# A block of attention, a state-space mixer and 32 experts: the first gather issued ahead of the low parts, masks behind the first four reciprocal roots

## The chip, the cores and the metric

The kernel runs on one core of a Trainium2 chip, in one launch. The metric is device time in microseconds (us). The five engines of the core are TensorE (PE in the profile), VectorE (DVE), ScalarE (ACT), GpSimd (POOL) and SyncE (SP, which here only issues loads); each runs its own list of instructions in order, and waits on semaphores for the others.

## The reference

The input is `x`, 1024 rows of 1024 numbers in float32. Cut to what is computed:

```python
h = rmsnorm(x, norm_mix_g)
q, k, v, f, u_ssm, g_attn, g_ssm = split(h @ w_in)         # 512 512 512 8 512 1024 1024
y_attn = forgetting_attention(rmsnorm(q), rmsnorm(k), v, f + b_forget)   # 8 heads of 64
y_ssm = s5(u_ssm, ...)                                     # 32 groups, state 64, GELU, GLU
mixed = sigmoid(g_attn) * (y_attn @ w_proj_attn) + sigmoid(g_ssm) * (y_ssm @ w_proj_ssm)
x = x + mixed @ w_out
xt = rmsnorm(x, norm_ffn_g)
# router: the best of 4 groups, in it the best 2 of 8 experts, weights renormalised
for e in range(32):
    y += combine[:, e:e+1] * ((silu(xt @ w_gate[e]) * (xt @ w_up[e])) @ w_down[e])
return x + y
```

Each expert has two matrices of 1024 x 256 and one of 256 x 1024, in all 3 MB in float32.

## The kernel before, in words

**Products.** Most products are made of three: a float32 operand is cast to a high part (ScalarE, names ending in `h`), and VectorE subtracts that from the operand to get the low part (names ending in `l`). TensorE then multiplies high by high, high by low and low by high into the same PSUM tile.

**The start (lines 95 to 262).** SyncE loads `x` in eight tiles of 128 rows, the first four ahead of `raw_u` (the weights of `u_ssm` and `f`, four loads), the last four (`xs2`) behind it. `normalize` (L176) takes four tiles: ScalarE squares and sums a tile (L180), VectorE makes the mean square `ss` (L181), GpSimd raises it to -1/2 (`rstd`, L183), VectorE scales the tile (L184). `split_u` (L193) makes `wuh`, `wul` and a small `wf`, which GpSimd clears first (L227). `turn_x` (L186) transposes four tiles on TensorE and splits the result into `hTh` (ScalarE, L190) and `hTl` (VectorE, L191). For the first half of the rows this stands in a manual schedule for ScalarE and VectorE; on the other engines, and elsewhere, a scheduler orders the instructions from their dependencies. The masks `tri`, `mask_s`, `mask_m` and three small vectors (L232 to L254) are made on GpSimd wherever it comes to them. The second half's `normalize(xs2)` is placed behind the last `hTl` of the first half by `tc.issue_after`, which orders instructions of one engine.

**The routing.** The last large product before the experts, `mixed @ w_out`, goes over 16 units (a tile of 128 rows, one half of the columns). Behind each unit `tail` (L1169) does the routing of a finished tile, mostly in small instructions of VectorE: best group, best two experts, and from comparisons and small products on TensorE a table `ptab` of which rows each expert takes. At the end VectorE writes `ix` (L1313), the row numbers of each of the 32 experts, 96 places each, and `wts` (L1314). The normalised rows go to a scratch tensor `xn_d` in HBM. `AHEAD` (L1126) says in which unit which loads of weights are issued: an expert has four loads of `raw_e` and two of `wd`, 512 KB each, in five sets of buffers, so that expert 5's `raw_e` waits until expert 0's buffers are read.

**The experts (from L1319).** `gather_rows` fetches an expert's rows from `xn_d` by `ix` into a tile `XG` with an indirect DMA that GpSimd issues (L1330); `XG` is cleared beforehand (`rows_tile`, L1321). `turn_rows` transposes the rows on TensorE (L1341) and splits them into `xh` and `xl` (L1344, L1345). `split_expert` splits an expert's gate and up weights into eight pieces, `weh` on ScalarE (L1103) and `wel` on VectorE (L1104). `gate_up` multiplies (L1354 to L1356), `hidden` applies SiLU (L1362), `down` multiplies by `wd` (L1379), scales (L1380) and adds the rows to the output with an indirect DMA (L1381). The three `XG` are used in turn; gather o + 2 is issued while expert o is multiplied.

Of the kernel before, what the change touches and what calls it, by code (L numbers as in the profile page):

```python
# [19 lines left out]
P = 128  # L20
# [22 lines left out]
def hybrid_block(ctx: ExitStack, tc: tile.TileContext, t, out):  # L43
# [132 lines left out]
    def normalize(xs):  # L176
        for x_ in xs:
# [5 lines left out]
            nc.gpsimd.tensor_tensor(rstd, ss, mhalf[:, 0:1], ALU.pow)  # L183
            nc.vector.tensor_scalar(x_, x_, rstd, None, op0=ALU.mult)  # L184

    def turn_x(xs, k, hs):  # L186
# [3 lines left out]
        nc.scalar.activation(hTh[k][:, hs], ps, AF.Copy, scale=gmix[:, k:k + 1])  # L190
        return nc.vector.scalar_tensor_tensor(hTl[k][:, hs], ps, gmix[:, k:k + 1], f32(hTh[k][:, hs]),  # L191
# [41 lines left out]
    tri = cp.tile([P, P], F32, name="tri")  # L233
    nc.gpsimd.memset(tri, 1.0)
    nc.gpsimd.affine_select(tri, tri, pattern=[[1, P]], compare_op=ALU.is_gt, fill=0.0,
                            base=0, channel_multiplier=-1)

    mask_s = cp.tile([P, 256], BF16, name="mask_s")
    nc.gpsimd.memset(mask_s, 0.0)
    nc.gpsimd.affine_select(mask_s, mask_s, pattern=[[1, 256]], compare_op=ALU.is_ge, fill=NEG,  # L240
                            base=-128, channel_multiplier=-1)

    mask_m = cp.tile([P, P], BF16, name="mask_m")
    nc.gpsimd.memset(mask_m, 0.0)
    nc.gpsimd.affine_select(mask_m, mask_m, pattern=[[-1, P]], compare_op=ALU.is_ge, fill=NEG,
                            base=0, channel_multiplier=1)
    bfor = cp.tile([H, 1], F32, name="bfor")
    nc.gpsimd.dma_start(bfor, t["b_forget"].rearrange("(p o) -> p o", o=1))

    gk2 = cp.tile([P, 1], F32, name="gk2")  # L250
    gqt = cp.tile([P, 1], F32, name="gqt")
    for o in (0, 64):
        nc.gpsimd.dma_start(gk2[o:o + 64], t["k_norm_g"].rearrange("(p o) -> p o", o=1))
        nc.gpsimd.dma_start(gqt[o:o + 64], t["q_norm_g"].rearrange("(p o) -> p o", o=1))  # L254
    xs = xs2
    pu, pf = [mmtile() for _ in range(4)], smtile()
    with tc.issue_after(first_half.ins):
# [833 lines left out]

    def split_expert(raws, c):
# [425 lines left out]
```

## Time and profile before

| | us |
|---|---|
| median of three runs | 1182.69 |
| the three runs | 1181.40, 1182.69, 1185.41 |
| the profiled execution, its own time | 1180.84 |
| its span in the trace | 1179.2 |
| TensorE busy | 1106.0 (94%) |
| VectorE busy | 804.9 (68%) |
| ScalarE busy | 620.3 (53%) |
| GpSimd busy | 356.9 (30%) |

The span runs from the first to the last instruction; 1.6 us of the execution lie around it. The mean granted clock of TensorE is 0.98 of full speed. Busy times overlap between engines. A time within the span is counted from its start.

### The profile page before, as it was taken

The numbers are of one execution on the slowest core, as the hardware profiler recorded it, in microseconds if no ns is written. First come the engines' busy times: TensorE is split into PE (matmuls) and PEld (weight loads), VectorE is DVE, ScalarE is ACT, GpSimd is POOL, SyncE is SP. The second block draws the span as 40 slices with busy tenths as digits, with TensorE's granted clock in tenths as the row PEclk, the third lists the DMA queues.
The fourth block names the chain that finished last, engine by engine and source line by source line (L and its number), as shares of the span: only waits on it lengthen the run. The fifth ranks groups of instructions, "written<-read, shape, count | busy, mean of one in ns | idle before, by whom it ended". The sixth has DMA issues, their size and how long they took to land. (4 is left out here: it accounts for less than half of the span.)

```text
span 1179.2 us, 15928 instructions
## 1 busy us (share of the span) xinstructions
PE 1106.0 (94%) x5323; PEld 848.4 (72%) x5324; DVE 804.9 (68%) x1593; ACT 620.3 (53%) x1195; POOL 356.9 (30%) x399
## 2 busy tenths in 40 slices
PE   5999999999999999999899979997699999999995
PEld 4778878887897888788677868885466666666562
DVE  4986887964247899898986795529466666666660
ACT  5443233234246666658868452204376776666662
POOL 3110111013144565647443451102322222222211
PEclk9999999999999999999999999998799999999998
DMA  7625553321604030002523548554599999999992
GB/s 237 88 75 149 130 82 82 81 73 49 152 22 55 11 64 11 16 10 81 205 81 135 184 170 295 181 208 183 188 331 345 327 315 305 314 317 322 311 331 56
DMA packets 100918, 193.78 MB, mean 164 GB/s; under 512 B 26176, under 2 KB 55168, under 8 KB 100832
## 3 DMA queue, kind: packets, MB, share of 16 engines
q1 hardware_dynamic: 82176, 150.16, 41.5%
q0 software_dynamic: 14048, 34.17, 10.6%
q10 hardware_dynamic: 4608, 8.39, 1.9%
q8 instruction: 43, 0.70, 0.2%
q14 instruction: 43, 0.35, 0.1%
HBM read 164.30 MB, written 35.52 MB: 169 GB/s over the span
## 5 line engine op out<-in xcount | busy, mean ns | idle before, releaser
L1104 DVE TENSOR_TENSOR wel<-raw_e,weh 128x512 fp32r<-128x512 f32 x256 | 157.5, 686 | 116.9 <-ACT weh L1103 116.9
L1103 ACT CAST weh<-raw_e 128x512 fp32r<-128x512 f32 x256 | 137.2, 622 | 2.2 <-DVE wel L1104 0.8
L1379 PE MATMUL psA_t<-wd,hT 128*96 128x512 f32 x256 | 115.7, 594 | 3.0 <-DMA wd<-in_w_expert_down 2.2
L912 POOL TENSOR_TENSOR sm<-sm,pe 128x256 f32<-128x256 f32 (+2 forms) x80 | 96.1, 1202 | 70.3 <-ACT pe L909 62.0
L1354 PE MATMUL psA_t<-weh,xh 128*96 128x512 f32 x256 | 103.8, 406 | 0.2
L1355 PE MATMUL psA_t<-wel,xh 128*96 128x512 f32 x256 | 102.2, 399 | 0.0
L1356 PE MATMUL psA_t<-weh,xl 128*96 128x512 f32 x256 | 101.3, 396 | 0.0
L162 PE MATMUL psA_t<-hTl,wgh 128*128 128x512 f32 x256 | 100.7, 393 | 0.0
L161 PE MATMUL psA_t<-hTh,wgl 128*128 128x512 f32 x256 | 100.7, 393 | 0.0
L160 PE MATMUL psA_t<-hTh,wgh 128*128 128x512 f32 x256 | 100.5, 393 | 0.0
L795 PE MATMUL psA_t<-wqh,hTh 128*128 128x384 f32 x256 | 88.0, 344 | 0.0
L796 PE MATMUL psA_t<-wql,hTh 128*128 128x384 f32 x256 | 86.4, 338 | 0.0
L797 PE MATMUL psA_t<-wqh,hTl 128*128 128x384 f32 x256 | 86.3, 337 | 0.0
L1381 POOL DMA_INDIRECT out_rows<-R,ix x32 | 46.0, 1438 | 127.3 <-ACT hT L1370 116.1
L1380 ACT ACTIVATE R<-psA_t,wts 96x512 f32<-96x512 f32 x64 | 43.7, 682 | 75.8 <-PE psA_t L1379 73.7
L1379 PEld LDWEIGHTS psA_t<-wd,hT 128*96 128x96 f32 x256 | 40.0, 167 | 55.0 <-issue 48.9
L1330 POOL DMA_INDIRECT XG<-xn_d,ix x32 | 35.8, 1119 | 139.0 <-PE psB_t L1341 133.1
L907 ACT ACTIVATE pH<-psB_t 128x512 fp32r<-128x512 f32 (+1 forms) x96 | 49.1, 511 | 36.4 <-PE psB_t L904 36.2
L910 DVE TENSOR_TENSOR pL<-pe,pH 128x256 fp32r<-128x256 f32 (+2 forms) x80 | 62.5, 793 | 6.5 <-ACT pe L909 5.7
L164 ACT COPY ge<-psA_t 128x512 f32<-128x512 f32 x32 | 18.7, 584 | 86.6 <-PE psA_t L162 81.8
L857 DVE TENSOR_REDUCE mx<-psB_t 128x1 f32<-128x512 f32 (+2 forms) x96 | 51.2, 551 | 6.2 <-PE psB_t L855 2.7
L1163 PE MATMUL psA_t<-woh,mxh 128*128 128x512 f32 x128 | 54.3, 424 | 1.2 <-DVE gt L988 1.2
(425 smaller groups left out, 2828.7 us busy)
## 6 DMA issues: line engine op xcount, KB each, us to landing
raw_e<-in_w_expert_gate SPq DMA_DIRECT2D x64, 512.0 KB
raw_e<-in_w_expert_up SPq DMA_DIRECT2D x64, 512.0 KB
wd<-in_w_expert_down SPq DMA_DIRECT2D x64, 512.0 KB
gate_d<-ge ACTq DMA_DIRECT2D x32, 256.0 KB
gt<-gate_d SPq DMA_DIRECT2D x16, 512.0 KB
raw_g<-in_w_in SPq DMA_DIRECT2D x12, 512.0 KB
raw_q<-in_w_in SPq DMA_DIRECT2D x48, 128.0 KB
x<-in_x SPq DMA_DIRECT2D x8, 512.0 KB
```

The lines of the kernel that those rows point to most:

```text
L160: nc.tensor.matmul(ps, wh, hTh[k][:, ns], start=(k == 0), stop=False)
L161: nc.tensor.matmul(ps, wl, hTh[k][:, ns], start=False, stop=False)
L162: nc.tensor.matmul(ps, wh, hTl[k][:, ns], start=False, stop=(k == KD - 1))
L795: nc.tensor.matmul(ps[:, :384], ah, wh, start=(k == 0), stop=False)
L796: nc.tensor.matmul(ps[:, :384], ah, wl, start=False, stop=False)
L912: nc.gpsimd.tensor_tensor(sm[:, o0:], sm[:, o0:], pe[:, :n], ALU.add)
L1103: nc.scalar.copy(wh[d_], src)
L1104: nc.vector.tensor_tensor(wl[d_], src, f32(wh[d_]), ALU.subtract)
L1354: nc.tensor.matmul(ps, xh[:, k, :], wh[:, k % 2, :], start=(k == 0), stop=False)
L1355: nc.tensor.matmul(ps, xh[:, k, :], wl[:, k % 2, :], start=False, stop=False)
L1356: last = nc.tensor.matmul(ps, xl[:, k, :], wh[:, k % 2, :], start=False, stop=(k == KD - 1))
L1379: pe = nc.tensor.matmul(po, hT[:, j, :], wd[j][:, ns], start=(j == 0), stop=(j == 1))
```

## The change

At the start:

- The clearing of `wf` and everything on GpSimd from `tri` to `gqt` is put behind the fourth `rstd` (`power`).
- `normalize(xs2)` is put behind the last `hTh` of the first half too, so that on ScalarE its four Squares come after all eight `hTh`.

At the border between routing and experts:

- `XG[0]` and `XG[1]` are cleared in unit 8 of the product loop instead of after it.
- Expert 2's two `wd` loads are issued after the loop instead of in unit 8.
- Expert 0's weights are split by a function of its own, `split_first`: all eight `weh` first, then `wel` in two groups of four. The first group stands behind `tick`, a one-column tile that GpSimd clears between gather 0 and gather 1 and VectorE copies onto itself; the second stands behind the second `xl` of expert 0's rows.

```diff
 def normalize(xs):
-            nc.gpsimd.tensor_tensor(rstd, ss, mhalf[:, 0:1], ALU.pow)
+            power = nc.gpsimd.tensor_tensor(rstd, ss, mhalf[:, 0:1], ALU.pow)
             nc.vector.tensor_scalar(x_, x_, rstd, None, op0=ALU.mult)
+        return power
...
-        normalize(xs)
-        nc.gpsimd.memset(f32(wf), 0.0)
+        power = normalize(xs)
+        with tc.issue_after(power.ins):
+            nc.gpsimd.memset(f32(wf), 0.0)
...
-            first_half = turn_x(xs, k, halves[0])
+            first_act, first_half = turn_x(xs, k, halves[0])
+    with tc.issue_after(power.ins):
...    (tri, mask_s, mask_m, bfor, gk2, gqt as before, indented)
-    with tc.issue_after(first_half.ins):
+    with tc.issue_after(first_half.ins), tc.issue_after(first_act.ins):
         normalize(xs)
...
+    def split_first(raws, c):
+        ws, low = [], []
+        for k2 in range(4):
+            v = (2 * c + k2 // 2) % 3, k2 % 2
+            ws_t[v] = slot("weh", (2, 512), F32R), slot("wel", (2, 512), F32R)
+            wh, wl = ws_t[v]
+            for q in range(2):
+                src = raws[k2 // 2 * 2 + q][:, k2 % 2 * 2:k2 % 2 * 2 + 2, :]
+                d_ = (slice(None), slice(None), slice(q * 256, q * 256 + 256))
+                nc.scalar.copy(wh[d_], src)
+                low.append((wl[d_], src, f32(wh[d_])))
+            ws.append((wh, wl))
+        for u in range(2):
+            yield ws
+            for l_ in low[4 * u:4 * u + 4]:
+                nc.vector.tensor_tensor(*l_, ALU.subtract)
+        yield ws
...
-    AHEAD = {0: [(0, 6)], 2: [(1, 6)], 8: [(2, 6)], 12: [(3, 6), (4, 2)], 14: [(4, 2)]}
+    AHEAD = {0: [(0, 6)], 2: [(1, 6)], 8: [(2, 4)], 12: [(3, 6), (4, 2)], 14: [(4, 2)]}
...
+            if u == 8:
+                rows_tile(SR)
+                rows_tile(SR)
...
         for _ in range(2):
+            next(ahead[2])
+        for _ in range(2):
             r_ = next(ahead[4])
...
-    rows_tile(SR)
-    rows_tile(SR)
...
-    for o in range(2):
-        last_gather = gather_rows(XG[o], icol(o))
+    tick = em_.tile([P, 1], F32, name="tick")
+    gather_rows(XG[0], icol(0))
+    nc.gpsimd.memset(tick, 0.0)
+    last_gather = gather_rows(XG[1], icol(1))
     with tc.issue_after(last_gather.ins):
         rows_tile(em_)
+    last_dve = nc.vector.tensor_copy(tick, tick)
...
-    with after(ends["act"], last_dve):
-        *_, ws = split_expert(got[0][0], 0)
+    with after(ends["act"]):
+        sp = split_first(got[0][0], 0)
+        ws = next(sp)
+    with after(last_dve):
+        next(sp)
+    x, _, dve = turn_rows(XG[0])
+    with after(dve):
+        next(sp)
     load(5, 4)
-    x, _ = turn_rows(XG[0])
```

`turn_x` and `turn_rows` now return the instructions that the new orders name (`act`, `dve`).

**GpSimd at the start.** The rows stand in the order of the engine; `x4` is four in a row. Before:

```order
L183 TENSOR_TENSOR rstd<-ss,mhalf 128x1
L234 MEMSET tri 128x128
L239 MEMSET mask_s 128x256
L235 AFFINE_SELECT tri<-tri 128x128
L240 AFFINE_SELECT mask_s<-mask_s 128x256
L244 MEMSET mask_m 128x128
L248 DMA bfor<-in_b_forget 8x1
```

and now:

```order
masks.py:199 AFFINE_SELECT ident<-ident 128x128
L183 TENSOR_TENSOR rstd<-ss,mhalf 128x1 x4
L229 MEMSET wf 128x1024
L237 MEMSET tri 128x128
L242 MEMSET mask_s 128x256
L238 AFFINE_SELECT tri<-tri 128x128
```

Before, masks and small DMAs lay between the roots, and the clearing of `wf` ahead of the first one; now the four roots follow each other, and the clearing of `wf` is the next instruction behind them.

**ScalarE at the start.** `x_109` to `x_115` are the four tiles of the second half, `hTh_136` to `hTh_141` the high parts of k = 2 to 7. Before:

```order
L190 ACTIVATE hTh_136<-psB_t,gmix 128x512
L180 ACTIVATE junk,ss<-x_109 128x1024
L190 ACTIVATE hTh_137<-psB_t,gmix 128x512
L180 ACTIVATE junk,ss<-x_111 128x1024
L198 CAST wuh<-raw_u 128x1024
L199 CAST wf<-raw_u 128x2x8
L190 ACTIVATE hTh_138<-psB_t,gmix 128x512
```

and now:

```order
L191 ACTIVATE hTh_136<-psB_t,gmix 128x512
L191 ACTIVATE hTh_137<-psB_t,gmix 128x512
L199 CAST wuh<-raw_u 128x1024
L200 CAST wf<-raw_u 128x2x8
L191 ACTIVATE hTh_138<-psB_t,gmix 128x512
```

The Square of `x_109` stood between the high parts of k = 2 and k = 3; now k = 3 follows k = 2 at once, and the four Squares stand behind `hTh_141`.

**VectorE from the list of rows to the first hidden values `hh`.** Before:

```order
L1313 TENSOR_TENSOR ix<-psA_t,empty 96x32
L1314 COPY wts<-psA_t 96x32
L1104 TENSOR_TENSOR wel<-raw_e,weh 128x2x256 x9
L1345 TENSOR_TENSOR xl<-psB_t,xh 128x384
L1104 TENSOR_TENSOR wel<-raw_e,weh 128x2x256
```

and now:

```order
L1346 TENSOR_TENSOR ix<-psA_t,empty 96x32
L1347 COPY wts<-psA_t 96x32
L1490 TENSOR_REDUCE nblk<-cnt 1x1
L1495 CAST cnti<-cnt 1x32
L1492 TENSOR_SCALAR nblk<-nblk 1x1
L1493 TENSOR_SCALAR nblk<-nblk 1x1
L1496 CAST cnti<-nblk 1x1
L1433 COPY tick<-tick 128x1
L1111 TENSOR_TENSOR wel<-raw_e,weh 128x2x256 x4
L1370 TENSOR_TENSOR xl<-psB_t,xh 128x384 x2
L1111 TENSOR_TENSOR wel<-raw_e,weh 128x2x256 x4
L1126 TENSOR_TENSOR wel<-raw_e,weh 128x2x256 x4
```

The nine `wel` behind `wts` became four, and these stand behind the copy of `tick`; the other four of expert 0 (L1111) stand behind both `xl`, and all four first ones of expert 1 (L1126) behind them. Five small operations on the experts' counts, which stood behind expert 1's `wel` before, now stand ahead of the tick. On GpSimd the same place now reads:

```order
L1304 TENSOR_TENSOR xn_8066<-xn_8066,gfB 128x512
L1355 DMA XG<-xn_d,ix 96x1024
L1429 MEMSET tick 128x1
L1355 DMA XG<-xn_d,ix 96x1024
L1158 MEMSET XG 128x1024
```

Before, the two clearings of `XG` stood between `xn` and the gathers, and the gathers of experts 0 and 1 followed each other.

On SyncE's queue the four `wd` loads (two of expert 2, two of expert 4) now stand between `xn_d` and the loads of expert 5, the first of them between the two halves of `xn_d`; before there were two, behind both halves.

## Rows read from the trace of the kernel before

**Rows 1.** The page of the profile, its first part: busy time of an engine, its share of the span, and its instructions.
```profile
PE 1106.0 (94%) x5323; PEld 848.4 (72%) x5324; DVE 804.9 (68%) x1593; ACT 620.3 (53%) x1195; POOL 356.9 (30%) x399
```

**Rows 2.** The table of windows over the border between routing and experts and over the experts. Columns: the window, its length, busy time and instructions of TensorE (PE), its weight loads (PEld), VectorE (DVE), ScalarE (ACT) and GpSimd (POOL), then the granted clock of TensorE as a share of full speed, the mean busy share of the 16 DMA engines, and what they moved in GB/s.
```profile
820.00:825.00 5.00, 1.54 (x7) 0.92 (x6) 4.34 (x26) 5.00 (x11) 0.63 (x1) 0.50 0.72 218
825.00:830.00 5.00, 0.00 (x0) 0.00 (x0) 3.99 (x7) 0.30 (x1) 4.97 (x1) 0.50 0.68 219
830.00:835.00 5.00, 0.00 (x0) 0.00 (x0) 0.00 (x0) 0.00 (x0) 2.92 (x3) 0.50 0.89 279
835.00:840.00 5.00, 3.52 (x13) 2.61 (x14) 2.02 (x4) 2.51 (x5) 0.96 (x1) 0.50 0.25 71
840.00:845.00 5.00, 5.00 (x18) 3.38 (x17) 1.35 (x7) 0.66 (x1) 0.00 (x0) 0.73 0.78 243
845.00:850.00 5.00, 4.88 (x27) 3.74 (x26) 2.95 (x6) 3.68 (x9) 0.95 (x1) 1.00 0.24 73
...
870.00:900.00 30.00, 30.00 (x127) 18.79 (x126) 18.58 (x34) 20.91 (x43) 7.24 (x6) 1.00 1.03 348
900.00:1100.00 200.00, 200.00 (x836) 125.30 (x835) 124.14 (x219) 139.39 (x278) 47.05 (x40) 1.00 0.99 318
```

**Rows 3.** The timeline of TensorE at the border. Columns of this and of all timelines below: start, duration, engine, line, operation, output<-inputs, shape, number of instructions, and in brackets the idle time before it with what ended it.
```profile
836.43 1.52 PE L1341 MATMUL psB_t<-ident,XG 96*128 96x96 f32 x8 [13.17 <-DMA XG<-xn_d,ix]
...
842.98 0.39 PE L1354 MATMUL psA_t<-weh,xh 128*96 128x512 f32 x1
```

**Rows 4.** The timeline of GpSimd at the border.
```profile
817.10 1.93 POOL L1323 MEMSET XG<- 128x1024 f32 x2
824.37 5.60 POOL L1330 DMA_INDIRECT XG<-xn_d,ix  x1 [5.34 <-DVE wel L1104]
830.27 0.99 POOL L1330 DMA_INDIRECT XG<-xn_d,ix  x1 [0.30 <-DMA raw_e<-in_w_expert_up]
...
838.23 0.96 POOL L1330 DMA_INDIRECT XG<-xn_d,ix  x1 [4.76 <-PE psB_t L1341]
```

**Rows 5.** The timeline of VectorE at the border: the list of rows, the burst of low parts, and the low part of the gathered rows.
```profile
823.30 0.19 DVE L1313 TENSOR_TENSOR ix<-psA_t,empty 96x32 int32<-96x32 f32 x1 [0.60 <-PE psA_t L1265]
...
823.50 5.49 DVE L1104 TENSOR_TENSOR wel<-raw_e,weh 128x512 fp32r<-128x512 f32 x9
837.98 0.56 DVE L1345 TENSOR_TENSOR xl<-psB_t,xh 128x384 fp32r<-128x384 f32 x1 [8.99 <-ACT xh L1344]
```

**Rows 6.** The timeline of VectorE a little earlier: the same comparison `at` for the last tile, first beside the clearings on GpSimd, then alone.
```profile
817.50 0.64 DVE L1264 TENSOR_SCALAR at<-iocap,pos 128x96 f32<-128x96 f32 x1
...
822.36 0.27 DVE L1264 TENSOR_SCALAR at<-iocap,pos 128x96 f32<-128x96 f32 x1
```

**Rows 7.** The instructions of line 1330, the gather, with the time from issue to landing: the first line is of the window that holds the first gather alone, the next two of the 29 from 836 on (durations in ns).
```profile
DMA to landing us min/median/max: 11.9/11.9/11.9
...
L1330 POOL DMA_INDIRECT XG<-xn_d,ix x29: 952/975/991, 838.2 to 1115.8; - x29
...
DMA to landing us min/median/max: 4.0/7.7/8.7
```

**Rows 8.** The timeline of SyncE's queue (SPq) at the border: loads of `wd` and of `raw_e`, 512 KB each.
```profile
819.08 0.83 SPq L1089 DMA_DIRECT2D wd<-in_w_expert_down  x2
825.41 0.33 SPq L1085 DMA_DIRECT2D raw_e<-in_w_expert_gate  x1
...
828.42 0.33 SPq L1085 DMA_DIRECT2D raw_e<-in_w_expert_up  x1
840.27 0.33 SPq L1085 DMA_DIRECT2D raw_e<-in_w_expert_gate  x1
```

**Rows 9.** The timeline of GpSimd at the start.
```profile
2.68 0.98 POOL L227 MEMSET wf<- 128x1024 f32 x1
...
12.15 0.52 POOL L254 DMA_DIRECT2D gqt<-in_q_norm_g  x1
12.69 0.57 POOL L183 TENSOR_TENSOR rstd<-ss,mhalf 128x1 f32<-128x1 f32 x1
```

**Rows 10.** The timeline of VectorE at the start: the mean square and the scaling of the fourth tile of x.
```profile
11.97 0.15 DVE L181 TENSOR_SCALAR ss<-ss 128x1 f32<-128x1 f32 x1
13.29 0.75 DVE L184 TENSOR_SCALAR x<-x,rstd 128x1024 f32<-128x1024 f32 x1 [1.17 <-POOL rstd L183]
```

**Rows 11.** The timeline of ScalarE at the start.
```profile
10.56 0.19 ACT L180 ACTIVATION_READ_ACCUMULATOR junk<-x 128x1 f32 x1
...
22.08 1.06 ACT L180 ACTIVATE junk<-x 128x1024 f32<-128x1024 f32 x1 [4.57 <-DMA x<-in_x]
...
23.13 0.67 ACT L190 ACTIVATE hTh<-psB_t,gmix 128x512 fp32r<-128x512 f32 x1
```

**Rows 12.** The timeline of TensorE at the start.
```profile
24.64 0.66 PE L189 MATMUL psB_t<-ident,x 128*128 128x128 f32 x4 [1.59 <-DVE hTl L191]
...
34.40 0.41 PE L189 MATMUL psB_t<-ident,x 128*128 128x128 f32 x2 [0.38 <-DVE x L184]
```

**Rows 13.** The waits between 1100 and 1140: who waited for what, us in total, times, the longest.
```profile
PE psA_t L1379 <- DMA wd<-in_w_expert_down: 2.2, 2, 1.9
...
ACT weh L1103 <- DMA raw_e<-in_w_expert_up: 0.7, 1, 0.7
ACT weh L1103 <- DMA raw_e<-in_w_expert_gate: 0.6, 1, 0.6
```

More of the change, by code (lines that the diff above doesn't have):

```diff
@@ L189, in turn_x @@
             nc.tensor.transpose(ps[:, r * P:(r + 1) * P], xs[r][:, k * P:(k + 1) * P], ident)
-        nc.scalar.activation(hTh[k][:, hs], ps, AF.Copy, scale=gmix[:, k:k + 1])
-        return nc.vector.scalar_tensor_tensor(hTl[k][:, hs], ps, gmix[:, k:k + 1], f32(hTh[k][:, hs]),
+        act = nc.scalar.activation(hTh[k][:, hs], ps, AF.Copy, scale=gmix[:, k:k + 1])
+        return act, nc.vector.scalar_tensor_tensor(hTl[k][:, hs], ps, gmix[:, k:k + 1], f32(hTh[k][:, hs]),
                                               op0=ALU.mult, op1=ALU.subtract)
@@ L230, in hybrid_block @@
                 split_u(k)
-            first_half = turn_x(xs, k, halves[0])
[L233 to L254, printed above, removed]
+            first_act, first_half = turn_x(xs, k, halves[0])
@@ new lines, in hybrid_block @@
+    with tc.issue_after(power.ins):
+        tri = cp.tile([P, P], F32, name="tri")
+        nc.gpsimd.memset(tri, 1.0)
+        nc.gpsimd.affine_select(tri, tri, pattern=[[1, P]], compare_op=ALU.is_gt, fill=0.0,
+                                base=0, channel_multiplier=-1)
+        mask_s = cp.tile([P, 256], BF16, name="mask_s")
+        nc.gpsimd.memset(mask_s, 0.0)
+        nc.gpsimd.affine_select(mask_s, mask_s, pattern=[[1, 256]], compare_op=ALU.is_ge, fill=NEG,
+                                base=-128, channel_multiplier=-1)
+        mask_m = cp.tile([P, P], BF16, name="mask_m")
+        nc.gpsimd.memset(mask_m, 0.0)
+        nc.gpsimd.affine_select(mask_m, mask_m, pattern=[[-1, P]], compare_op=ALU.is_ge, fill=NEG,
+                                base=0, channel_multiplier=1)
+        bfor = cp.tile([H, 1], F32, name="bfor")
+        nc.gpsimd.dma_start(bfor, t["b_forget"].rearrange("(p o) -> p o", o=1))
+        gk2 = cp.tile([P, 1], F32, name="gk2")
+        gqt = cp.tile([P, 1], F32, name="gqt")
+        for o in (0, 64):
+            nc.gpsimd.dma_start(gk2[o:o + 64], t["k_norm_g"].rearrange("(p o) -> p o", o=1))
+            nc.gpsimd.dma_start(gqt[o:o + 64], t["q_norm_g"].rearrange("(p o) -> p o", o=1))
@@ L1131, in hybrid_block, with rows_tile @@
     cnt = rp.tile([P, NE], F32, name="cnt")
+    XG = []
+    def rows_tile(where):
+        XG.append(slot("XG", where=where) if where is SR else where.tile([P, S], F32, name="XG"))
+        nc.gpsimd.memset(XG[-1], 0.0)
     ptab = mmtile()
@@ L1318, in hybrid_block @@
     em_ = pool(ctx, "moe", 1, side="right")
-    XG = []
-    def rows_tile(where):
-        XG.append(where.tile([P, S], F32, name="XG") if where is em_ else slot("XG", where=where))
-        nc.gpsimd.memset(XG[-1], 0.0)
-    rows_tile(SR)
-    rows_tile(SR)
     mt = pool(ctx, "moet", 2, side="right")
@@ L1344, in turn_rows @@
             nc.scalar.copy(xh[dst], pv)
-            nc.vector.tensor_tensor(xl[dst], pv, f32(xh[dst]), ALU.subtract)
-        return (xh, xl), pe
+            dve = nc.vector.tensor_tensor(xl[dst], pv, f32(xh[dst]), ALU.subtract)
+        return (xh, xl), pe, dve
     def gate_up(x, ws):
```

2 lines of the change are left out of this document (1 added, 1 removed).

## The prediction

> **What bounds the kernel now.** I read the page first: TensorE is busy 94% of the span [rows 1], so time can only come out of the few stretches in which it stands still, and anything that does not shorten one of them is worth nothing. The slices show two such stretches that the change touches: the first 40 us, and the border between the routing and the experts. The table of windows gives the second its size: between 825 and 835 TensorE does nothing, and its clock stands at 0.50 until 840 [rows 2]. The waits and the timeline name the cause: the first transposes of the experts start at 836.43 after 13.17 us of waiting for the gathered rows of expert 0 [rows 3].
>
> Why are those rows late? `ix`, the list of rows, starts on VectorE at 823.30, and the gather starts on GpSimd at 824.37. It then takes 5.60 us to issue; each of the later 29 takes 0.95 to 0.99 [rows 4, 7]. What differs is VectorE: it runs nine low parts (`wel`) back to back from 823.50, 5.49 us, to 828.99 [rows 5]. The gather ends at 829.97, which is 828.99 plus one normal issue of 0.98. I read this as the issue being held until VectorE's burst ends. The gather at 838.23 is the counter-sample: it ran beside an `xl`, which has one input in PSUM, and took 0.96 [rows 4].
>
> Then come the packets: 11.9 us from the start of the issue to landing, against 4.0 at the least and 7.7 in the middle later on [rows 7]. Without the hold, 11.9 would be 11.9 - 5.60 + 0.96 = 7.3, still long; meanwhile four 512 KB loads of expert 5, released by the same nine `wel`, went out from 825.41 to 828.42 [rows 8], ahead of the packets.
>
> From 870 on TensorE is busy all the time, but so are the DMA engines: share 1.03, then 0.99 [rows 2]. Between 1100 and 1140 TensorE and ScalarE at last wait for weights, 2.2 us for `wd`, 0.7 and 0.6 for `raw_e` [rows 13]. The load stream has thus just been caught up there; a start that is earlier for TensorE alone would be waited back. This matters below.
>
> **The change part by part.**
>
> *The gather.* The four `wel` of the first half of expert 0 now stand behind a tick that GpSimd writes after gather 0, so VectorE holds nothing that long when it issues. `ix` was finished at 823.49, 0.88 before the issue; with the correction below it is finished at 823.2. A later gather followed its releaser by 0.28 (transposes to 837.95, gather at 838.23 [rows 3, 4]). So the issue starts between 823.5 and 824.1, takes 0.96, and the rows land 4.0 to 7.3 us after its start: 827.5 to 831.4, against 836.3. Which end? For the early one speaks that the four loads of expert 5 no longer go ahead; for the late one that two more `wd` loads (1 MB) are now issued at the border: four of 512 KB from about 819, at the 348 GB/s of [rows 2] 6.0 us, so that the queues are busy until about 826. I take 823.8 and 5.5 us, near the middle: landing at 829.3, TensorE 7.0 us earlier, range 4.9 to 8.8. The matmuls behind it run at the low clock at first, before and after alike (clock 0.50 in 835 to 840, 0.73 in 840 to 845 [rows 2]); nothing is gained or lost there.
>
> A page speaks against this term. The Trainium skill, page "SBUF — State Buffer", section "Who interferes with whom", infers that a `tensor_tensor` does not hold up descriptor generation, since it takes only the read interface of the port that VectorE and GpSimd share. By that rule the 5.60 us would belong to the gather itself and stay. No run here shows the issue without the burst, so the rule keeps a rival of its own.
>
> *What the delayed low parts cost.* First four: behind the tick, about 825.0 to 827.4, hidden under the landing. Second four: behind both `xl`. `xl` starts 1.55 us after the transposes (837.98 against 836.43 [rows 3, 5]) and two of them end about 2.6 after; four `wel` of 0.61 (5.49 / 9) end at 5.1. TensorE came to its 13th matmul, the first that needs them, at 842.98, 6.55 after the transposes [rows 3]. Covered by 1.4 us: nothing.
>
> *Loads.* Expert 5's second pair (1 MB) and expert 2's two `wd` (1 MB) now fall between 819 and the saturated stretch: 6.0 us of DMA time. The share between 820 and 850 leaves 5 x (0.28 + 0.32 + 0.11 + 0.75 + 0.22 + 0.76) = 12.2 us idle [rows 2]. If TensorE starts 7.0 earlier, the stream has to start 7.0 earlier too, and 1 MB more (the `wd`; 3.0 us) has to fit: 10.0 of the 12.2 idle must be used. I see about 3 us that can't be (waits for the second `wel` group and for expert 1's), so I charge +0.8. Ends: 0 and +3.0.
>
> *Two clearings of `XG`.* Taken away behind `xn` (1.93 us at 817.10 [rows 4]). VectorE's `at` took 0.64 beside them, 0.27 alone [rows 6]; with its neighbours I take -0.3 on `ix` (0 to -0.6). In the product loop they cost GpSimd 1.93 us beside a TensorE that is busy throughout: nothing; if an `rstd` waits, 0.97.
>
> *The start.* The root of tile 3 starts at 12.69, behind masks and small DMAs, though the last square is read out at 10.75 [rows 9, 11]. With the masks gone: 10.75, then `ss` 0.15 [rows 10] and the root 0.57 make 11.5, against 13.26. But the clearing of `wf` (0.98 [rows 9]) now stands right behind that root. It takes GpSimd first, and VectorE's scaling of x is a form with one input, as `at` was when it waited for the clearings [rows 6]. So x starts at about 12.5 instead of 13.29 [rows 10]: -0.8; bounds -1.8 (no hold) and 0 (the second `raw_u` is awaited instead).
>
> *ScalarE's order.* The Square of x's fifth tile waited 4.57 us for its load and ran at 22.08; hTh of k = 3 stood behind it and came at 23.13, and TensorE stood for 1.59 at 24.64 [rows 11, 12]. All hTh now go first: -1.5. The four Squares follow them together, so x's second half should be scaled sooner than before, and the 0.38 that TensorE waited for it at 34.40 [rows 12] goes as well: -0.3. The start is worth -2.6, from -0.5 to -4.
>
> **Sum**: -7.0 + 0.8 - 0.3 - 2.6 = -9.1 us. On the profiled execution's 1180.84 that is 1171.7; this execution lies 1.85 below the median, so the median goes from 1182.69 to about **1173.6**. A measurement here tells about 0.3%, 3.5 us, from no change.
>
> **The rivals.**
>
> *The first gather is slow of itself.* Its issue stays 5.6, from 823.8 to 829.4; the queues are then free, so the packets take about 3 (4.0 - 0.96): landing at 832.4, -3.9 instead of -7.0, with the loads in step. Sum -3.9 - 0.3 - 2.6 = -6.8: 1176. For it: it is the first of 32 and the only slow one. Against it: its end falls within 0.02 us of where the burst's end puts it. The rule of the Trainium skill named above would give the same time. 17%.
>
> *The load stream decides the end.* If little of the idle time can be used, for instance because expert 5's second pair waits for `xl`, the gain at the border is waited back between 1100 and 1140: -7.0 becomes -4.0, at worst -2.0. Sum -6.9 to -4.9: 1176 to 1178. For it: shares of 0.99 and 1.03 and the waits in [rows 13]. Against it: the loads are released by the same `wel`, which come earlier with TensorE. 18%.
>
> *Slower.* One mechanism: gather 0 lands no earlier, since the four `wd` loads lie ahead of it, and the second group of `wel` waits for it. Then expert 5's second pair leaves at 841 instead of 828, beside expert 6's pair (840.27 [rows 8]); the stream enters the saturated stretch up to 6.0 us (2 MB) behind, and TensorE waits that at the end. 6.0 - 2.6 - 0.3 = +3.1: 1186. It decides from a landing later than about 834.5. Against it: 2 MB issued at 819 should be through by 826. 6%.
>
> *It doesn't do what it says*: VectorE's five small operations for `cnti`, which now come before the tick, or the tick itself, hold the gather as the `wel` did, or the start's gain is waited for on `raw_u`. Sum 1180 to 1183. 7%.
>
> **How the numbers follow.** Forecast 52% (1169 to 1176); the first two rivals 35%, mostly faster by more than 3.5 us; no effect 7%, slower 6%. So faster 0.82, same 0.12, slower 0.06. The range reaches from the forecast's low end (-8.8 - 0.6 - 4 + 0 = -13.4, 1169) to the load rival's worst with the start at its lower bound (-2.0 - 0.3 - 0.5 = -2.8, 1180).
>
> **What would show it.** Right: the first gather at about 1 us, TensorE's wait for `XG` 5 to 9 us, landing near 829; GpSimd's fourth root before 12; no stall of TensorE at 24; a wait for `wd` after 1100 of at most 3 us more. Wrong: a first gather of 5 us beside an idle VectorE; TensorE's wait above 10; or a border that is 7 us shorter with weight waits after 1100 that are 5 us longer.

## The result, and the profile after

| us | before | after |
|---|---|---|
| median of the comparison's runs (four each) | 1183.51 | 1169.25 |
| their range | 1181.40 to 1185.41 | 1166.55 to 1170.91 |
| profiled execution | 1180.84 | 1170.50 |
| its span | 1179.2 | 1168.8 |

The ratio is 0.988, 95% interval 0.9858 to 0.9902: 11.6 to 16.8 us faster. The forecast was 1173.6, the range 1169 to 1180. The two profiled executions stand 10.34 apart, the medians 14.26: the profiled run of before lay 2.67 below its median, that of after 1.25 above its own (10.34 + 2.67 + 1.25 = 14.26). Every term below is read from these two profiles.

Four marks on the profiles cut the difference of the spans, 10.4 us, into pieces (starts of instructions):

| from, to | before | after | change | forecast |
|---|---|---|---|---|
| start to the last large product before the experts | 811.98 | 808.49 | -3.5 | -2.6 (start) |
| from there to `ix` | 11.32 | 10.96 | -0.4 | -0.3 (clearings) |
| `ix` to the first transposes of the experts | 13.13 | 6.64 | -6.5 | -7.0 (gather) |
| from there to the end | 342.8 | 342.7 | -0.1 | +0.8 (loads) |

**The border.** First TensorE, as in [rows 3]: start, duration, engine, line, operation, shape, number, and in brackets the idle time before it.

```profile
826.09 1.52 PE L1366 MATMUL psB_t<-ident,XG 96*128 96x96 f32 x8 [6.68 <-DMA XG<-xn_d,ix]
827.66 0.74 PE L1379 MATMUL psA_t<-weh,xh 128*96 128x512 f32 x1
```

The wait for the rows is 6.68 us instead of 13.17. Behind it no row of TensorE up to 834 carries an idle time: the second group of low parts, which now waits for `xl`, is covered, as forecast. GpSimd, against [rows 4]:

```profile
819.93 1.11 POOL L1355 DMA_INDIRECT XG<-xn_d,ix  x1 [6.26 <-DVE nblk L1490]
821.05 0.12 POOL L1429 MEMSET tick<- 128x1 f32 x1
821.34 1.50 POOL L1355 DMA_INDIRECT XG<-xn_d,ix  x1 [0.18 <-issue]
```

VectorE, against [rows 5]:

```profile
819.45 0.19 DVE L1346 TENSOR_TENSOR ix<-psA_t,empty 96x32 int32<-96x32 f32 x1 [0.61 <-PE psA_t L1293]
...
821.20 0.15 DVE L1433 COPY tick<-tick 128x1 f32<-128x1 f32 x1 [0.77 <-issue]
821.28 2.50 DVE L1111 TENSOR_TENSOR wel<-raw_e,weh 128x512 fp32r<-128x512 f32 x4
827.63 1.08 DVE L1370 TENSOR_TENSOR xl<-psB_t,xh 128x384 fp32r<-128x384 f32 x2 [3.86 <-ACT xh L1369]
```

The first gather is issued in 1.11 us instead of 5.60, and the low parts begin 0.24 us after its end. The second gather is worth a look: it starts 0.06 us into a burst of four low parts and takes 1.50, not the 3.4 that the end of the burst plus 0.98 would give. That did not fit my theory, and the experiments below are about it. The landing of the first gather, against [rows 7] (11.9):

```profile
DMA to landing us min/median/max: 6.0/6.0/6.0
```

SyncE's queue, against [rows 8]:

```profile
814.11 0.38 SPq L1092 DMA_DIRECT2D wd<-in_w_expert_down  x1
...
815.59 1.43 SPq L1092 DMA_DIRECT2D wd<-in_w_expert_down  x3
823.20 0.33 SPq L1088 DMA_DIRECT2D raw_e<-in_w_expert_gate  x1
823.81 0.33 SPq L1088 DMA_DIRECT2D raw_e<-in_w_expert_up  x1
830.58 0.33 SPq L1088 DMA_DIRECT2D raw_e<-in_w_expert_gate  x1
```

The four `wd` loads go ahead of the gather; expert 5's second pair leaves only at 830.58, behind its packets. The table of windows, columns as in [rows 2]:

```profile
820.00:825.00 5.00, 0.00 (x0) 0.00 (x0) 2.94 (x8) 0.41 (x1) 4.54 (x5) 0.50 0.79 266
825.00:830.00 5.00, 3.86 (x14) 2.81 (x15) 2.37 (x5) 2.84 (x6) 1.00 (x2) 0.50 0.91 259
830.00:835.00 5.00, 5.00 (x22) 3.52 (x21) 3.52 (x6) 1.48 (x2) 0.00 (x0) 0.89 0.88 245
835.00:840.00 5.00, 4.88 (x27) 3.69 (x27) 3.88 (x8) 4.61 (x10) 0.96 (x1) 1.00 0.84 288
840.00:845.00 5.00, 5.00 (x23) 3.13 (x22) 3.88 (x8) 2.88 (x7) 0.96 (x1) 1.00 0.86 278
```

One stretch of standing still is left where there were two, and the DMA share stays at 0.79 to 0.91 where it fell to 0.25 and 0.24 before [rows 2]: of the 12.2 us of idle DMA time that the prediction counted there, these windows still have 3.6 (5 x 0.72). The late waits (all that TensorE and ScalarE wait for weights after 840), against [rows 13] (2.2, 0.7 and 0.6):

```profile
PE psA_t L1404 <- DMA wd<-in_w_expert_down: 2.0, 1, 2.0
ACT weh L1125 <- DMA raw_e<-in_w_expert_up: 1.5, 1, 1.5
```

Together 3.5 as before: in this profile nothing was waited back.

**The start.** GpSimd and VectorE, against [rows 9, 10]:

```profile
11.15 0.55 POOL L183 TENSOR_TENSOR rstd<-ss,mhalf 128x1 f32<-128x1 f32 x1 [0.93 <-DVE ss L181]
11.64 0.95 POOL L229 MEMSET wf<- 128x1024 f32 x1
```

```profile
11.73 1.55 DVE L184 TENSOR_SCALAR x<-x,rstd 128x1024 f32<-128x1024 f32 x1 [0.66 <-POOL rstd L183]
```

The fourth root comes 1.54 us earlier, and the scaling behind it takes 1.55 instead of 0.75 beside the clearing of `wf`: held by 0.8, as forecast, so that x is done at 13.28 instead of 14.04. The waits of TensorE in the first 70 us (who waited for what: total, times, longest), of before and of after:

```profile
PE psB_t L189 <- DVE ss L181: 9.9, 3, 7.5
PE psB_t L189 <- DVE hTl L191: 1.6, 1, 1.6
PE psB_t L189 <- DVE x L184: 1.3, 2, 0.9
PE psA_t L208 <- DVE hTl L191: 1.0, 1, 1.0
PE psA_t L206 <- ACT uS L221: 1.0, 1, 1.0
```

```profile
PE psB_t L190 <- DVE x L184: 8.9, 3, 7.4
PE psB_t L190 <- DVE ss L181: 1.1, 1, 1.1
PE psA_t L207 <- ACT uS L222: 0.5, 1, 0.5
PE psA_t L207 <- DVE uS L220: 0.2, 1, 0.2
```

14.8 against 10.7. The stall of 1.6 at 24 [rows 12] is gone, and so is a wait of 1.0 for another `hTl` that the forecast did not count.

### The profile page after: what moved, and what is told of

Its sections match the earlier page's. It is cut to its first block, busy times and chain, and to the rows that moved or that the text cites. A ratio compares the mean times of both kernels' runs of the same rounds, so it can differ in the third digit from the quotient of the medians.

```text
span 1168.8 us, 15930 instructions
## 1 busy us (share of the span) xinstructions
PE 1106.3 (95%) x5323; PEld 848.5 (73%) x5324; DVE 805.0 (69%) x1594; ACT 620.4 (53%) x1195; POOL 353.4 (30%) x400
## 5 line engine op out<-in xcount | busy, mean ns | idle before, releaser
L1126 DVE TENSOR_TENSOR wel<-raw_e,weh 128x512 fp32r<-128x512 f32 x248 | 152.3, 685 | 118.3 <-ACT weh L1125 114.5
L1125 ACT CAST weh<-raw_e 128x512 fp32r<-128x512 f32 x248 | 132.7, 623 | 1.6 <-DMA raw_e<-in_w_expert_up 1.5
L1355 POOL DMA_INDIRECT XG<-xn_d,ix x32 | 32.1, 1002 | 136.3 <-PE psB_t L1366 129.6
L161 PEld LDWEIGHTS psA_t<-hTh,wgl 128*128 128x128 f32 x256 | 48.1, 188 | 9.7
L160 PEld LDWEIGHTS psA_t<-hTh,wgh 128*128 128x128 f32 x256 | 48.1, 188 | 9.6
```

What stands on the lines that cost most here:

```text
L160: nc.tensor.matmul(ps, wh, hTh[k][:, ns], start=(k == 0), stop=False)
L161: nc.tensor.matmul(ps, wl, hTh[k][:, ns], start=False, stop=False)
L1125: nc.scalar.copy(wh[d_], src)
L1126: nc.vector.tensor_tensor(wl[d_], src, f32(wh[d_]), ALU.subtract)
```

## The experiments

The theory: the issue of a gather is held until VectorE's burst of low parts ends, and takes 0.98 us from there. Its rival: the first gather is slow of itself. Twelve kernels, from their profiles and times ("burst": start, duration and number of the low parts that gather 0 meets; the two columns from the trace are starts of instructions and the span's end):

| kernel | time (runs), ratio to before | gather 0 issue | burst | `ix` to transposes | transposes to end |
|---|---|---|---|---|---|
| before | 1183.51 (4) | 5.60 | 823.50 5.49 x9 | 13.1 | 342.8 |
| after | 1169.25 (4), 0.988 | 1.11 | none | 6.6 | 342.7 |
| start_alone | 1179.56 (12), 0.9981 | 5.61 | 821.12 5.49 x9 | 12.8 | 346.0 |
| border_alone | 1173.43 (7), 0.992 | 1.10 | none | 8.4 | 344.4 |
| no_tick_8 | 1170.98 (1) | 1.47 | 819.47 4.91 x8 | 5.9 | 344.2 |
| no_tick_4 | 1173.97 (1) | 1.55 | 820.92 2.50 x4 | 6.0 | 345.7 |
| xg_border_no_tick | 1178.48 (1) | 1.58 | 826.65 4.90 x8 | 8.1 | 342.5 |
| xg_border_tick | 1182.86 (1) | 1.11 | none | 5.2 | 348.0 |
| late_gather | 1177.68 (1) | 1.12 | 823.57 4.91 x8 | 10.2 | 342.5 |
| wd_early | 1179.13 (1) | 2.89 | 826.00 2.48 x4 | 9.7 | 342.1 |
| wd_late_only | 1191.33 (6), 1.0085 | 7.42 | 828.99 7.30 x12 | 15.7 | 343.1 |
| wd_twice | 1190.30 (1) | 5.61 | 826.01 5.49 x9 | 16.1 | 346.6 |
| wf_early | 1171.18 (6), 0.9895 | 1.11 | none | 6.7 | 344.7 |
| nblk_first | 1176.28 (6), 0.9942 | 1.58 | 822.91 5.51 x9 | 8.0 | 343.0 |

In no_tick_8, late_gather and xg_border_no_tick one, two and four low parts of expert 1 follow the eight at once. A time of one run can't be told from another one within some 5 us (the runs of before lie between 1177.4 and 1187.6); the profile's durations can.

**Each half alone.** `start_alone`: the start of the change, the border of before.

```diff
+        power = normalize(xs)
+        with tc.issue_after(power.ins):
+            nc.gpsimd.memset(f32(wf), 0.0)
...
-    with tc.issue_after(first_half.ins):
+    with tc.issue_after(first_half.ins), tc.issue_after(first_act.ins):
         normalize(xs)
```

> The kernel before with the start part alone (wf and masks behind the four roots, the second half's Squares behind all hTh). Theory: the start is worth the 3.5 us by which TensorE's last large product ended earlier in the changed kernel (811.98 to 808.49), so the time falls by 3 to 4.5 us against before, and the border keeps its 13.2 us wait and its 5.6 us gather. Rival: the start's gain is waited back later (clock, loads), time within 2 us of before.

`border_alone`: the other half.

```diff
-    AHEAD = {0: [(0, 6)], 2: [(1, 6)], 8: [(2, 6)], 12: [(3, 6), (4, 2)], 14: [(4, 2)]}
+    AHEAD = {0: [(0, 6)], 2: [(1, 6)], 8: [(2, 4)], 12: [(3, 6), (4, 2)], 14: [(4, 2)]}
...
+            if u == 8:
+                rows_tile(SR)
+                rows_tile(SR)
...
+    gather_rows(XG[0], icol(0))
+    nc.gpsimd.memset(tick, 0.0)
+    last_gather = gather_rows(XG[1], icol(1))
...
+    last_dve = nc.vector.tensor_copy(tick, tick)
+    with after(ends["act"]):
+        sp = split_first(got[0][0], 0)
```

> The kernel before with the border part alone (tick, low parts in two groups, clearings in the product loop, two wd loads later). Theory: -6.5 us for the gather and -0.4 for the list of rows, 6 to 8 us less than before; TensorE's wait for the rows 6.5 to 7 us, the start as before (first product at 15.3, a stall of 1.6 near 24.6). Rival: the shortened wait depends on the earlier start too, or is waited back for weights after 1100: less than 4 us. If the two parts add up to more than 11 us, the medians (-14.3) tell more than the trace (-10.4).

By the medians the start is worth 3.2 us (1179.56 against 1182.72), by the ratio 2.2 (0.9981, interval 0.9965 to 0.9998, so 0.2 to 4.1 us); the border is worth 9.3 (0.992, 0.990 to 0.994), more than the 6 to 8 expected. Together 12.4 by the medians; the whole change gave 14.3, 11.6 to 16.8. TensorE's waits in the first 70 us are 10.7 in start_alone and 14.1 in border_alone. Gather 0 takes 5.61 and 1.10: the border's edit alone frees it. The profile of border_alone is of its slowest run (1178.67; the other six lie between 1172.0 and 1173.9), so its stretches are read with care.

The border's gain in `ix`, read as -0.4 in after, seems to be missing in border_alone: from the last large product to `ix` it has 11.26, before 11.32. Cut at `gm`, a step of the routing of the last tile on VectorE, the gain is there. The same step before, in after, and in border_alone with its `ix`:

```profile
817.11 0.15 DVE L1213 MAX8 gm<-lg 128x8 f32<-128x8 f32 x1
```

```profile
813.62 0.16 DVE L1241 MAX8 gm<-lg 128x8 f32<-128x8 f32 x1
```

```profile
818.27 0.15 DVE L1238 MAX8 gm<-lg 128x8 f32<-128x8 f32 x1
...
824.10 0.19 DVE L1343 TENSOR_TENSOR ix<-psA_t,empty 96x32 int32<-96x32 f32 x1 [0.61 <-PE psA_t L1290]
```

From `gm` to `ix`, where the clearings lay, it is 6.19 before and 5.83 in after and in border_alone. Four more kernels that clear at the border have 6.18 or 6.19 (start_alone, xg_border_no_tick, wd_late_only, nblk_first), four more that clear in the loop 5.82 or 5.83 (no_tick_8, no_tick_4, late_gather, wf_early); the remaining three have other waits in this stretch. What border_alone loses lies ahead of `gm`: TensorE's last products of the router take 0.92 us there instead of 0.62.

**The tick taken away.** If the burst holds the gather, the tick must be what saves it.

```diff
-    last_dve = nc.vector.tensor_copy(tick, tick)
...
-    x, _, dve = turn_rows(XG[0])
-    with after(dve):
         next(sp)
+    x, _, dve = turn_rows(XG[0])
```

> The changed kernel without the copy of the tick: all eight low parts of expert 0 directly behind the list of rows. Theory (the gather is held until VectorE's burst of two-input subtractions ends): burst 819.7 to 824.6 or 825.2 with a ninth, first gather ends about 1 us after it, 5 to 5.6 us long; TensorE's wait 10 to 12.5 us. Rival (the first gather was slow because of what else lay there, as the loads or the clearings just before it): first gather at 1 to 1.6 us in spite of the burst, wait below 8 us.

`no_tick_4` takes out only the first line, and so keeps groups of four.

> The changed kernel without the copy of the tick, low parts in two groups of four, the first four directly behind the list of rows. Theory (held until the burst ends): four subtractions end near 822.3, the first gather ends about 1 us later, 3 to 3.5 us long; TensorE's wait about 8.5 to 9.5 us. Rival (any overlap costs the full 4.6 us, or one subtraction only as the second gather of the changed kernel, 1.50 us, suggests): 5.6 us, or 1.5 us.

Both went against the theory; for no_tick_4 the time of one subtraction, 1.5, had been named beside it. VectorE and GpSimd in no_tick_8:

```profile
819.36 0.17 DVE L1488 TENSOR_REDUCE nblk<-cnt 1x1 f32<-1x32 f32 x1
819.47 4.91 DVE L1111 TENSOR_TENSOR wel<-raw_e,weh 128x512 fp32r<-128x512 f32 x8
```

```profile
819.67 1.47 POOL L1355 DMA_INDIRECT XG<-xn_d,ix  x1 [6.37 <-DVE nblk L1488]
```

These eight end at 824.38, so the theory puts the gather's end at 825.36 at the earliest, and it was 821.14. That is the end of the one low part that ran when the gather started (819.47 + 0.69 = 820.16) plus 0.98. The burst is there, the gather starts inside it as in before, and it is held for one instruction, not for eight.

**The clearings put back at the border**, without the tick and with it. To keep GpSimd's order, gather 0, the tick's clearing and gather 1 are tied to each other.

```diff
-            if u == 8:
-                rows_tile(SR)
-                rows_tile(SR)
...
+    rows_tile(SR)
+    rows_tile(SR)
...
-    gather_rows(XG[0], icol(0))
-    nc.gpsimd.memset(tick, 0.0)
+    first_gather = gather_rows(XG[0], icol(0))
+    with after(first_gather):
+        first_tick = nc.gpsimd.memset(tick, 0.0)
...
```

> The kernel without the copy of the tick, and with the first two clearings of XG back behind xn at the border; the low parts stand directly behind the list of rows, here twelve in a row. The same without the moved clearings (no_tick_8) had a first gather of 1.47 us in spite of eight low parts beside it. Theory now (the place of the clearings decides, with the burst): first gather long again, and if it is held until the burst ends, about 7.5 to 8 us long, since twelve of 0.60 run 7.3 us. Rival A (a fixed cost of the first gather where the clearings stand before it): 5.6 us whatever the burst. Rival B (neither; the number of waits or loads in the old kernel): 1 to 1.6 us.

> The changed kernel with the first two clearings of XG back behind xn at the border, low parts still behind the tick. Theory (a long first gather needs both the clearings right before it and the burst beside it): first gather about 1.1 us, TensorE's wait 6 to 7.5 us, time within 1 us of the changed kernel's. Rival A (the clearings alone, without any burst, make the first gather long): 5.6 us, and the low parts, which wait for the tick, come 4.5 us later, wait about 11 us. The list of rows should come about 0.35 us later than in the changed kernel in either case.

Neither shows the hold: 1.58 beside the burst, 1.11 without one. So the place of the clearings does not decide it. Both times are worse for another reason: TensorE waits 4.2 us for `xT` near 733, in the product loop, and its last large product starts some 6.5 us later than in after. VectorE's copy of `xT` stands behind an `xn` there, and that waits for an earlier store of `xn` to land (xg_border_no_tick; in after the `xn` at 726.00 has no such wait):

```profile
730.86 1.28 DVE L1298 SCALAR_TENSOR_TENSOR xn<-x,rstd,gfB 128x1024 f32<-128x1024 f32 x1 [5.64 <-DMA xn_d<-xn]
```

xg_border_tick and wd_late_only have the same wait (5.64 and 5.56); why it comes in these three is not shown. In xg_border_tick the rows land 4.0 us after the issue starts, the best of all, and the time from the transposes to the end is 348.0, the longest.

**The gather in the middle of a burst.** A copy of one element of the first low part on GpSimd, ahead of gather 0, makes it start while the burst is running.

```diff
+        late = nc.gpsimd.tensor_copy(tick, f32(ws[0][1])[:, 0, 0:1])
+        with after(late):
+            last_gather = gather_rows(XG[0], icol(0))
```

> The changed kernel without the tick; eight low parts directly behind the list of rows; on GpSimd a one-column copy of the first low part's result stands ahead of the first gather, so that it starts in the second low part instead of in the first, as in the kernel before (0.86 us behind the burst's start). Clearings in the product loop. Theory (place of the clearings): first gather 1.5 us. Rival (what decides is at which point of the burst the gather starts): held until the burst ends, 4.5 to 6 us.

It starts at 825.36 in a burst of eight from 823.57, in the third low part and not in the second as meant, and takes 1.12. Not held either.

**The loads.** `wd_early` is after, with expert 2's `wd` loads back in unit 8.

```diff
-    AHEAD = {0: [(0, 6)], 2: [(1, 6)], 8: [(2, 4)], 12: [(3, 6), (4, 2)], 14: [(4, 2)]}
+    AHEAD = {0: [(0, 6)], 2: [(1, 6)], 8: [(2, 6)], 12: [(3, 6), (4, 2)], 14: [(4, 2)]}
...
-        for _ in range(2):
-            next(ahead[2])
```

> The changed kernel with expert 2's two wd loads back in unit 8 of the product loop, so that two instead of four 512 KB loads lie ahead of the first gather. Theory (queues busy until the wd are through): the rows land 4 to 5 us after the issue starts instead of 6 to 7, TensorE's wait 4.5 to 5.5 us instead of 6.68, time 1 to 2 us less. Rival: the landing does not hang on the wd loads; the wait stays within 0.5 us of 6.68. Second rival: what is gained is waited back for weights after 1085 no more than before, since 1 MB less has to be loaded after the border.

`wd_late_only` makes the opposite move in the kernel before.

> The kernel before with one edit: expert 2's two wd loads issued after the product loop instead of in unit 8. No tick, clearings at the border, low parts (twelve in a row here) directly behind the list of rows. Across the runs so far the first gather was held until the burst of low parts ended in every kernel with two wd loads at the border (5.60, 5.61 and 2.89 us), and for one low part at most in every kernel with four (1.10 to 1.58 us). Theory: it is these two loads, so the first gather takes 1.1 to 1.6 us here, TensorE waits 8 to 9.5 us instead of 13.2, and the time falls by 4 to 5 us against before. Rival: the loads only coincide, and the tick or the clearings matter; the first gather takes about 8 us (twelve low parts of 0.60, and 1) and the time does not fall.

`wd_twice` is before with two of the `wd` loads at the border issued a second time.

```diff
+        wd4 = t["w_expert_down"][ORDER[4]].rearrange("(p j) f -> p j f", j=2)
+        for j in range(2):
+            tc.keep_in_program_order(nc.sync.dma_start(r_[1][j], wd4[:, j, :]))
```

> The kernel before with expert 4's two wd loads issued a second time into the same tiles (same data), so that the load queues are busy for 1 MB longer at the border, with every buffer where it was. Theory A (what frees the first gather is that weight loads are still running when it is issued): first gather 1.1 to 1.6 us. Theory B (what changed is which buffers XG and wd got, which the order of the loads also decides): first gather 5.6 us as before. Either way the rows can land late, behind 1 MB more.

In wd_early the scheduler put the tick's clearing ahead of gather 0, so the four low parts ran beside the gather. VectorE and GpSimd:

```profile
825.83 0.15 DVE L1431 COPY tick<-tick 128x1 f32<-128x1 f32 x1
825.91 0.16 DVE L1488 TENSOR_REDUCE nblk<-cnt 1x1 f32<-1x32 f32 x1
826.00 2.48 DVE L1111 TENSOR_TENSOR wel<-raw_e,weh 128x512 fp32r<-128x512 f32 x4
```

```profile
825.70 0.10 POOL L1427 MEMSET tick<- 128x1 f32 x1 [7.18 <-ACT weh L1105]
826.57 2.89 POOL L1353 DMA_INDIRECT XG<-xn_d,ix  x1 [0.77 <-DVE nblk L1488]
```

Burst to 828.48, gather to 829.46: end plus 0.98, held. With the hold back, this run can't answer what it was made for, how the `wd` loads change the landing; and its `ix` comes 17.5 us behind the last large product instead of 11.0, so its time is not the hold's alone. In wd_late_only twelve low parts came in a row:

```profile
829.85 7.42 POOL L1332 DMA_INDIRECT XG<-xn_d,ix  x1 [5.33 <-DVE wel L1104]
```

Burst to 836.29, gather to 837.27: again 0.98. wd_twice (831.50 to 832.48) and start_alone (826.61 to 827.59) give the same number. So five kernels have the hold (before, start_alone, wd_early, wd_late_only, wd_twice), with four, nine and twelve low parts: its length is the burst's, and the first half of the theory stands. More loads make the packets late (landing 14.9 us after the issue's start in wd_twice, 11.9 before) but the issue no longer. The move of the `wd` loads alone costs 8 us of the median (1183.27 beside it), but most of that is not at the border: in its profile the last large product starts 5.5 us later than before, with the wait for `xT` named above, and the way from `ix` to the transposes, with twelve low parts in a row, is 2.6 longer.

**One instruction.** What the kernels with the hold share: the first low part follows the copy `wts`, or, in wd_early, an `nblk` that waits for nothing. In those without it (both no_tick kernels, xg_border_no_tick, late_gather) it follows an `nblk` that first waits on semaphores. The group of `nblk` by its line shows it (durations in ns, first and last start; DVEq is VectorE's sequencer), in late_gather, then in wd_early, where no semaphore row stands beside it:

```profile
L1491 DVEq EVENT_SEMAPHORE  x3: 21/50/50, 823.2 to 823.4; - x3
```

```profile
L1488 DVE TENSOR_REDUCE nblk<-cnt x1: 164/164/164, 825.9 to 825.9; 1x1 f32<-1x32 f32 x1
```

So, in before, the small reduction `nblk`, which stood behind the low parts, is moved between `wts` and the nine low parts.

```diff
+    nblk = em_.tile([1, 2], F32, name="nblk")
+    with after(last_dve):
+        first = nc.vector.tensor_reduce(nblk[:, 0:1], cnt[0:1, :], axis=AX.X, op=ALU.max)
-    with after(ends["act"], last_dve):
+    with after(ends["act"], first):
         *_, ws = split_expert(got[0][0], 0)
...
-    nblk = em_.tile([1, 2], F32, name="nblk")
-    nc.vector.tensor_reduce(nblk[:, 0:1], cnt[0:1, :], axis=AX.X, op=ALU.max)
```

> The kernel before with one edit: the maximum of the experts' counts (nblk, one 0.17 us reduction of VectorE on one partition, which waits for GpSimd's earlier work) stands between wts and the burst of nine low parts instead of behind them. So far the first gather was held until the burst's end wherever the burst's first low part ran 669 to 677 ns, and for one low part only wherever it ran 691 to 693 ns; most kernels of the second kind had this reduction, or the tick, with its wait for GpSimd directly ahead of the burst. Theory: what VectorE does directly ahead of the burst decides; here first low part 692 ns, first gather 1.1 to 1.6 us, TensorE's wait 8 to 9.5 us instead of 13.2, time 4 to 5 us below before. Rival: that is not enough (the place of the tick on GpSimd, or buffers, or the start matter): first gather 5.6 us, wait 13, time within 1 us of before.

VectorE, GpSimd and TensorE in nblk_first:

```profile
822.64 0.18 DVE L1314 COPY wts<-psA_t 96x32 f32<-96x32 f32 x1
822.80 0.17 DVE L1415 TENSOR_REDUCE nblk<-cnt 1x1 f32<-1x32 f32 x1
822.91 5.51 DVE L1104 TENSOR_TENSOR wel<-raw_e,weh 128x512 fp32r<-128x512 f32 x9
```

```profile
823.60 1.58 POOL L1330 DMA_INDIRECT XG<-xn_d,ix  x1 [5.33 <-DVE wel L1104]
```

```profile
830.54 1.51 PE L1341 MATMUL psB_t<-ident,XG 96*128 96x96 f32 x8 [8.05 <-DMA XG<-xn_d,ix]
```

The same nine low parts, the gather 0.69 us into them (0.87 in before), and its issue falls from 5.60 to 1.58: the second low part ends at about 824.20, plus 0.98 is 825.18, the gather's end. The ratio is 0.9942 (0.9919 to 0.9964): 7.0 us of the median (4.3 to 9.6) from the place of one reduction of 0.17 us. Its profile shows 5.1 of them at the border (8.0 from `ix` to the transposes instead of 13.1). The bursts differ in their own durations too. The group of the low parts (ns, least, middle, most), in before, in nblk_first and in xg_border_no_tick:

```profile
L1104 DVE TENSOR_TENSOR wel<-raw_e,weh x9: 677/679/681, 823.5 to 828.3; 128x512 fp32r<-128x512 f32 x9
```

```profile
L1104 DVE TENSOR_TENSOR wel<-raw_e,weh x9: 685/687/693, 822.9 to 827.7; 128x512 fp32r<-128x512 f32 x9
```

```profile
L1111 DVE TENSOR_TENSOR wel<-raw_e,weh x8: 679/681/692, 826.6 to 830.9; 128x512 fp32r<-128x512 f32 x8
```

All nine of nblk_first are some 8 ns longer than those of before, but that is not the mark of the short form: in xg_border_no_tick, whose gather is held for one low part only, all but the first take 679 to 683, as in the kernels with the hold. What differs in all ten kernels is the first low part of the burst: 669 to 677 ns in the five with the hold, 692 or 693 in the five without.

**The clearing of `wf`.** It holds the fourth tile's scaling in after; `wf_early` puts it back ahead of the first root.

```diff
-        with tc.issue_after(power.ins):
-            nc.gpsimd.memset(f32(wf), 0.0)
+        nc.gpsimd.memset(f32(wf), 0.0)
```

> The changed kernel with wf cleared ahead of the first root, as before the change, and the masks left behind the fourth root. Theory: the scaling of the fourth tile takes 0.75 instead of 1.55 us, TensorE's first product starts 0.8 us earlier (13.8 instead of 14.59), and the time is 0.5 to 1 us below the changed kernel's, 11 to 15 us below before. Rival: the second raw_u load or the cast of wf takes over as what is awaited, no gain (first product within 0.2 us of 14.59).

The scaling takes 0.91 instead of 1.55, and the first large product comes 2.80 us after the root's start instead of 3.44. But the root itself came 0.4 later in this run, and the time is 1171.18, ratio 0.9895 (0.9874 to 0.9916), against 0.988 for the change; the expected 0.5 to 1 us less than the change can't be seen in the time.

## Why the prediction was right, step by step

**The gather: the size was right, the mechanism was half of it.** Forecast -7.0, measured -6.5 in after, -6.4 in wf_early and -4.8 in border_alone (8.4 left of 13.1; its rows landed 7.8 us after the issue's start, 6.0 in after). The issue started 0.29 us behind `ix` and landed in 6.0 where I had 5.5. The step "VectorE holds the issue until its burst ends" is exact to 0.01 us in five kernels. It is not enough: five others run such a burst beside the gather, and it is held for one low part at most. I had read one row, 5.60, and one counter-sample with a PSUM input, and drew from them a rule on the burst; the counter-sample that was missing is a burst of the same form with something else ahead of it. The tick did what it says, and was not needed in the place that it has: no_tick_8 has a wait of 5.9 without it.

The rule weighed against it, of the Trainium skill (page "SBUF — State Buffer", section "Who interferes with whom"), infers that a `tensor_tensor` does not hold descriptor generation up. The runs differ: 5.60, 7.42 and 2.89 us beside bursts of nine, twelve and four, and four of the five short cases (1.47 to 1.58, against 1.10 or 1.11 with no burst) wait for the low part that is running.

**The rivals.** A slow first gather is refuted: 1.11 us for the first of 32 in after. So is the slower case: with four `wd` loads ahead of it the gather still landed at about 826. And the small operations for `cnti` and the tick did not hold it.

**The load stream**: +0.8 forecast, -0.1 measured, late waits 3.5 and 3.5. Over the fourteen profiles the time from the transposes to the end lies between 342.1 and 348.0 with no order by how early TensorE starts (344.2 at 824.97, 346.6 at 841.87); one profile of a kernel can't tell a cost of 0.8 there. The late waits scatter as much: 3.5 in before and after, 8.5 in border_alone, 11.7 in start_alone.

**The clearings**: -0.4 for -0.3. The step is shown: `gm` to `ix` is 0.36 shorter in all six kernels that clear in the loop and keep their other waits.

**The start**: -2.6 forecast. Its time does not say that this was too little (start_alone: -3.2 by the medians, -2.2 by the ratio, -2.4 at the last large product of its profile, against -3.5 in after); TensorE's waits up to 70 fell by more, 4.1. The root's part came out to the digit (-0.8). Of the 4.1, 1.2 are waits for normalised x and 1.6 the stall at 24, both near their terms; what was missed is a second wait for `hTl` (1.0) and part of one for `uS` (0.3) that went with the first. How much of it is left at 808 one profile can't say: among the five kernels with the start of before, TensorE comes to the first transposes of x in the product loop between 704.5 and 709.0, among the nine with the new start between 700.5 and 704.5.

**The sum** was -9.1, and the profiles have -10.4: so far it is the terms that came out. The medians have -14.3, more than the best that its terms add up to (-13.4), and 1169.25 lies at the very end of the range. That the median fell inside is in part luck. The other 4 us are, in the arithmetic, where the two profiled runs lie among their like; no term explains them. The four runs of after list mean granted clocks of TensorE of 0.986, 0.984, 0.981 and 0.979 with times of 1166.55, 1168.00, 1170.50 and 1170.91, so the spread between them goes along with the clock; which of the two sets the other is not shown.

## What to carry to other kernels

A DMA that GpSimd issues beside a burst on VectorE should be looked at in the trace by itself: if its issue ends one normal issue after the burst's end, put it ahead of the burst, or see what stands directly ahead of the burst. Before a rule is drawn from one slow row, find a row with the same neighbours and another predecessor. And an edit that frees an issue pays only as far as the queues let the packets through: 1.1 to 1.6 us of issue were followed by landings from 4.0 to 7.9.

## What was not expected of the hardware

The hold has two forms. With the low parts directly behind a copy, or behind a reduction with no semaphore to wait for, the indirect DMA was held to the end of the whole burst plus 0.98 us, in five kernels of five, for four to twelve instructions. Directly behind a small instruction that had waited on semaphores, it was not held to the burst's end, in five of five: in four of them its end is the end of the single low part that was running plus 0.98, and in late_gather (1.12) no hold can be seen. The second gather of after (1.50), behind the copy of the tick, is of the short kind too. The rule was read from nine of these kernels; one, nblk_first, was forecast by it. The number of instructions, the place of the clearings, more loads and the phase do not decide it; late_gather and wd_early start at the same phase of a low part, and take 1.12 and 2.89. In the short form the first low part takes as long as one that starts behind an idle VectorE later on (691 to 695 ns in every kernel). Whether it is the wait or something else in the predecessor that sets the burst's form stays open: no kernel here keeps `nblk` in its place and takes the wait from it within an otherwise equal order, other than wd_early, where the `wd` loads and the tick's place differ too.
